# Five edits to a two-layer hybrid trunk: a later pump for the S5 sums, another PSUM pool, splits on another engine, compressed scores from split keys

## The chip, the core and the metric

The kernel runs on one core of one Trainium2 chip. Its engines have names in what follows: PE (TensorE, the matmuls; PEld is its weight load), DVE (VectorE), ACT (ScalarE), POOL (GpSimd) and SP (SyncE, which issues the DMAs). SBUF is the memory on the chip that the engines read and write, and PSUM, with eight banks, is where matmuls put their sums. The metric is the device time of one execution in microseconds (us).

## What is computed

Two layers of a decoder trunk, with a width of 1024 and 256 tokens. In each layer one input projection of the normed input feeds four token mixers; each mixer's output is gated, projected to 1024 and summed with the others:

```python
for l in range(DEPTH):
    h = rms_norm(x, norm_g[l])
    proj = h @ w_in[l]
    (nsa_q, nsa_kv, nsa_gate, nsa_z, sc_bcx, sc_z, sb_qkv, sb_z,
     s5_u, s5_z, merge) = jnp.split(proj, split_at, axis=-1)
    outs = (nsa_mixer(...) * jax.nn.silu(nsa_z), short_conv_mixer(...) * jax.nn.silu(sc_z),
            stick_breaking_mixer(sb_qkv) * jax.nn.silu(sb_z), s5_mixer(...) * jax.nn.silu(s5_z))
    gates = jax.nn.sigmoid(merge).reshape(b, s, N_MIXERS, D_MODEL)
    mixed = gates[:, :, 0] * (outs[0] @ w_branch[l, 0])
    for m in range(1, N_MIXERS):
        mixed = mixed + gates[:, :, m] * (outs[m] @ w_branch[l, m])
    x = x + mixed @ w_out[l]
```

Two of the mixers matter here. `nsa_mixer` is sparse attention; its compressed branch scores the queries against a few keys, each made of 32 tokens. `s5_mixer` is a complex linear recurrence over the 256 tokens, followed by a product with `c_re` and `c_im` that sums over the states. Weights and activations are float32.

## The kernel before

**Weights.** All projection weights come in 156 slots of 128x1024 (78 in each layer), in the order of use. SP issues one DMA for a slot (`raw`, three buffers). The slot is then split for products with more than one pass: `hi` is a cast to the format fp32r (L148, on ACT, for slots 17 and 87 on DVE), `lo` is `raw` minus `hi` (L150). The engine of L150 is DVE, save for the slots in the tuple `lo_pool`, where it is POOL. `hi` and `lo` have five buffers each. A product then has three passes: hi with hi, hi with lo, lo with hi, for the activations (`hh`, `hl`) as for the weights. `proj_n` (L488) and `proj_t` (L498) do so for 24 matmuls of 128x256 in each output bank or half bank.

**Stages of a layer.** First the slots of the queries and keys (`q`, `ksw`), the values `vsw`, the compressed keys `kvc`, the stick-breaking inputs (`sbq`, `sbk`, `sbv`), the S5 input `s5u` and the convolution's inputs; then merge gates (`mg`, four slots for each of eight blocks), SiLU gates (`z`) and the branch products (`br`, L943, one slot for each block) mixed as a list `TAIL` says, and at last the output product `wo`. A merge gate's tanh is L928 on ACT, and the gated branch products are the DVE operation `mt`, L946. POOL adds them up (L286).

**Order.** The mixers are Python generators. After each unit of projection the main program calls `pump()`, and every generator that isn't waiting is run on to its next `yield`; `yield n` sits out `n` pumps. So the code's order is that of the pumps. A scheduler with a model of the times then orders the instructions of PE, DVE and ACT, within what buffers and data allow. POOL and SP keep the order of the code.

**S5.** `s5` works on eight blocks of 128 states in a layer, two pairs with four blocks; a block is called a state below. For each state PE computes an input `bu`; DVE multiplies it with tables into `s5a` and `s5b` (L858, L859), POOL adds and subtracts halves (L286, L289), DVE scans along the tokens (L865, two scans), multiplies with the tables again into `cy` (L868, L871), POOL again subtracts and adds (L289, L286). After the four states of a pair comes a wait of two pumps and the sum over states, eight matmuls `s5acc` (L883). After the second pair come the weights of the last product (`gw`, a DMA, a cast and a subtraction on POOL) and the product `glu`. Names have the layer and the state at their end: `cy03` is state 3 of layer 0.

**PSUM pools.** `pj` has four banks, for projections; `wk` two, for mixers; `ac` two, for sums that live long (`s5acc` is one). Every projection of `n_part`, `ksw` too, takes a bank of `pj`.

**Compressed scores.** `nsa_compress` transposes the normed block-diagonal keys and copies them from PSUM as `bdkT`, in F32. `nsa_cmp` multiplies `hi` and `lo` of the queries with it: two matmuls for each of two token tiles and two head groups, eight in a layer, in F32 (L666).

## Time and profile before

| | before |
|---|---|
| three runs | 566.71, 568.88, 569.79 us (median 568.88) |
| the profiled execution | 566.94 us |
| its span, first to last instruction | 565.2 us |
| mean granted clock of PE, share of full speed | 0.987 |
| busy us: PE, DVE, ACT, POOL | 546.1, 440.1, 264.0, 275.3 |
| weight splits `lo` on DVE | 152, 209.1 us |
| weight splits `lo` on POOL | 4, 10.3 us |

All terms are worked out from the profiled execution, and 1.7 us of its time lie outside the span. The views that the prediction uses are: the busy shares of the engines (Rows 1), the list of PE's waits (Rows 2), which says who released PE after each wait, timelines of an engine over a few microseconds, and the busy time and granted clock of a stretch. In a timeline a row may stand for several like instructions ("x4"); the first number is the start of the first, the second the time from there to the end of the last. Matmuls overlap: a duration of 0.28 us is not what a matmul costs, that is the distance to the next start.

### The profile page before, as it was taken

Reading aid. Unit: us, or ns where it says so; the run is one execution under the profiler, and the core shown is the slowest. Engines: PE = TensorE matmul, PEld = TensorE weight load, DVE = VectorE, ACT = ScalarE, POOL = GpSimd, SP = SyncE. Lnnn points to the kernel's source line nnn. Section 1 sums busy time; section 2 is a strip of 40 time slices with the busy share of each in tenths; the row PEclk is TensorE's granted clock in tenths of the full one; section 3 lists DMA queues with packets and bytes.
Section 4 is the critical chain, followed back from the end, with each engine's and each line's share of the span. In section 5 each row is a group of like instructions: output and inputs, shape, how many; then the busy total and the mean of one; then the engine's idle time right before and its main releaser. Section 6 shows DMA issues by size and latency. Waiting matters only on the chain.

```text
span 565.2 us, 11178 instructions
## 1 busy us (share of the span) xinstructions
PE 546.1 (97%) x4417; PEld 510.1 (90%) x4417; DVE 440.1 (78%) x654; ACT 264.0 (47%) x436; POOL 275.3 (49%) x309
## 2 busy tenths in 40 slices
PE   6999999999899899799999999999999999999997
PEld 3898988889799799799998998889889999999997
DVE  3999776888989764888769985968898777687772
ACT  4656353654334444654454555454434345444440
POOL 7949536634665529597033776713335620243200
PEclk7899999999899999999999999999999999999999
DMA  7584154544444636465556725364344635555541
GB/s 257 194 279 157 42 201 119 199 153 146 150 126 137 223 134 206 149 199 180 190 171 213 220 72 164 112 222 135 112 154 147 202 139 180 187 188 186 188 135 53
DMA packets 28853, 93.54 MB, mean 166 GB/s; under 512 B 3968, under 2 KB 5248, under 8 KB 28800
## 3 DMA queue, kind: packets, MB, share of 16 engines
q1 hardware_dynamic: 28800, 92.82, 50.5%
q8 instruction: 35, 0.57, 0.4%
q14 instruction: 18, 0.15, 0.1%
HBM read 88.61 MB, written 1.05 MB: 159 GB/s over the span
## 4 chain that ended last, share of the span: by engine, by line
PE 71%; DVE 11%; POOL 9%; issue 4%; DMA 2%; ACT 2%; SPq 1%; DVEq 0%; POOLq 0%; ACTq 0%
PE mg L498 24%; PE wo L488 7%; PE br L943 7%; PE z L498 4%; DVE lo L150 2%; PE s5u L498 2%; PE sbv L488 2%; PE bg L498 2%; PE sc L709 2%; PE xin L498 2%; PE sbk L498 2%; PE nsacc L746 2%; DVE s5b L865 1%; POOL cy L286 1%; PE cg L498 1%
## 5 line engine op out<-in xcount | busy, mean ns | idle before, releaser
L150 DVE TENSOR_TENSOR lo<-raw,hi 128x1024 fp32r<-128x1024 f32 (+1 forms) x152 | 209.1, 1379 | 43.8 <-ACT hi L148 43.4
L148 ACT CAST hi<-raw 128x1024 fp32r<-128x1024 f32 (+1 forms) x154 | 161.2, 1050 | 173.8 <-PE mg L498 52.8
L498 PE MATMUL mg<-hh,hi 128*128 128x256 f32 x512 | 145.1, 283 | 0.4 <-DVE mt L946 0.4
L498 PE MATMUL mg<-hh,lo 128*128 128x256 f32 x512 | 144.6, 283 | 0.0
L498 PE MATMUL mg<-hl,hi 128*128 128x256 f32 x512 | 144.5, 282 | 0.0
L498 PEld LDWEIGHTS mg<-hh,hi 128*128 128x128 f32 x512 | 97.0, 190 | 3.0 <-issue 2.4
L498 PEld LDWEIGHTS mg<-hl,hi 128*128 128x128 f32 x512 | 97.4, 190 | 1.2 <-issue 1.2
L498 PEld LDWEIGHTS mg<-hh,lo 128*128 128x128 f32 x512 | 97.0, 189 | 1.2 <-issue 1.2
L286 POOL TENSOR_TENSOR mt<-mt,mt 128x512 f32<-128x512 f32 x12 | 19.0, 1585 | 70.6 <-DVE mt L946 70.6
L289 POOL TENSOR_TENSOR cy<-cy 128x256 f32<-128x256 f32 x16 | 18.2, 1138 | 57.9 <-DVE cy L871 54.2
L488 PE MATMUL wo<-hi,mx 128*128 128x256 f32 x256 | 45.6, 281 | 0.0
L488 PEld LDWEIGHTS wo<-hi,mx 128*128 128x128 f32 x256 | 39.2, 188 | 0.0
L943 PE MATMUL br<-oh,hi 128*128 128x256 f32 x128 | 36.0, 282 | 2.4 <-ACT g L928 2.4
L498 PE MATMUL z<-hh,hi 128*128 128x256 f32 x128 | 36.1, 282 | 0.0
L498 PE MATMUL z<-hl,hi 128*128 128x256 f32 x128 | 36.1, 282 | 0.0
L498 PE MATMUL z<-hh,lo 128*128 128x256 f32 x128 | 36.0, 281 | 0.0
L943 PE MATMUL br<-ol,hi 128*128 128x256 f32 x128 | 36.0, 281 | 0.0
L943 PE MATMUL br<-oh,lo 128*128 128x256 f32 x128 | 36.0, 281 | 0.0
L488 PE MATMUL wo<-lo,mx 128*128 128x256 f32 x128 | 35.3, 282 | 0.0
L865 DVE TENSOR_TENSOR_SCAN s5b<-r,s5a 128x256 f32<-128x256 f32 x32 | 20.3, 677 | 11.8 <-POOL s5a L289 11.8
L286 POOL TENSOR_TENSOR s5a<-s5a,s5b 128x256 f32<-128x256 f32 x16 | 20.2, 1262 | 17.1 <-DVE s5b L859 17.1
L943 PEld LDWEIGHTS br<-oh,hi 128*128 128x128 f32 x128 | 24.1, 189 | 2.6 <-ACT g L928 2.6
(333 smaller groups left out, 1417.4 us busy)
## 6 DMA issues: line engine op xcount, KB each, us to landing
raw<-in_ws_dram SPq DMA_DIRECT2D x152, 512.0 KB, 3.7
raw<-in_wq_dram SPq DMA_DIRECT2D x4, 536.0 KB, 5.0
w<-in_w_dram SPq DMA_DIRECT2D x4, 512.0 KB, 5.7
b<-bh SPq DMA_DIRECT2D x16, 64.0 KB, 2.0
u<-uh SPq DMA_DIRECT2D x16, 64.0 KB, 2.0
gw<-in_gw_dram SPq DMA_DIRECT2D x2, 512.0 KB, 5.4
out_dram<-xs SPq DMA_DIRECT2D x8, 128.0 KB, 1.7
xs<-in_x_dram SPq DMA_DIRECT2D x2, 256.0 KB, 3.2
```

Of the source, the lines that this page charges most:

```text
L148: self.nc.scalar.copy(hi[:, :w], t[:, :w])
L150: sub.tensor_sub(lo[:, :w], t[:, :w], hi[:, :w].bitcast(F32))
L286: G.tensor_add(o, a, b)
L289: G.tensor_sub(o, a, b)
L488: T.matmul(ps[:, :width], lhsT=act(4 * h + kk)[ia][:, tt], rhs=w[iw][:, kk, :], start=n == 0, stop=n == last)
L498: T.matmul(ps, lhsT=w[:, k, :], rhs=a[:, k, :], start=n == 0, stop=n == last)
L709: T.matmul(sc[kh].rearrange("p (b g k) -> p b g k", b=nb, g=2)[:, :, g, :], lhsT=qT[iq][rows[kh], g, t * P:(t + 1) * P], rhs=kT[ik][rows[k ...
L746: T.matmul(acc[rows[kh], :, t * P:(t + 1) * P], lhsT=v[:, c, b * P + 64 * kh:b * P + 64 * kh + 64], rhs=ps4[kh][:, c, 2 * i:2 * i + 2, :], ...
L865: V.tensor_tensor_scan(y[:, ri, :], L["r"][:, pr:pr + 1].to_broadcast([P, S]), a[:, ri, :], 0.0, op0=ALU.mult, op1=ALU.add)
L943: T.matmul(ps[:, j, :], lhsT=w[:, 2 * m + k, :], rhs=a[:, k, :], start=n == 0, stop=n == 5)
```

## The change

Five places of the code are changed.

1. `lo_pool` is empty: the splits of slots 4, 79, 81 and 95 are made by DVE.
2. `n_part` takes the bank of `ksw` from `ac`, of the others from `pj` as before.
3. `bdkT` becomes a pair of fp32r tiles, a rounded copy (ACT) and what the rounding leaves (one new subtraction of 128x64 on DVE).
4. The compressed scores are twelve fp32r matmuls in a layer, three passes, where eight F32 matmuls were.
5. In layer 0 the wait ahead of each pair's state sums is three pumps where two were; in layer 1 it stays at two (`3 - l`).

```diff
-    W = Weights(nc, tc, raw, hip, lop, wq, ws, 3, 5, (4, 79, 81, 95), (17, 87))
+    W = Weights(nc, tc, raw, hip, lop, wq, ws, 3, 5, (), (17, 87))
...
     def n_part(l, key, slots, act, t, done, width=256, by_pass=False):
-        ps = pj.tile([P, 512], F32, tag="pj", name=f"{key}{l}{t}")
+        pool, tag = (ac, "ac") if key == "ksw" else (pj, "pj")
+        ps = pool.tile([P, 512], F32, tag=tag, name=f"{key}{l}{t}")
...
-        bdkT = lp.tile([P, 64], F32, name=f"bdkT{l}", tag="bdkT")
-        A.copy(bdkT, pt[:, :64])
+        bdkT = tuple(lp.tile([P, 64], F32R, name=f"bdkT{i}{l}", tag=f"bdkT{i}") for i in range(2))
+        A.copy(bdkT[0], pt[:, :64])
+        V.tensor_sub(bdkT[1], pt[:, :64], bdkT[0].bitcast(F32))
...
-                for i in range(2):
-                    T.matmul(sc[:, t, g, :], lhsT=qT[i][:, g, t * P:(t + 1) * P].bitcast(F32), rhs=L["bdkT"], start=False,
-                             stop=t == g == i == 1)
+                for i, (iq, ik) in enumerate(PASSES):
+                    T.matmul(sc[:, t, g, :], lhsT=qT[iq][:, g, t * P:(t + 1) * P], rhs=L["bdkT"][ik], start=False,
+                             stop=t == g == 1 and i == 2)
...
-            yield 2
+            yield 3 - l
```

The scheduler answers with another order on PE, DVE and ACT. Three places of it carry the prediction. Lines of the code after stand one or two further down than before.

On PE, the last of the second pair's state sums in layer 0. `z30` is half of SiLU gate 3, which stands ahead of merge gate block 4 (`mg040`). Before:

```order
L498 MATMUL z30_2427<-hh0_154,hi45_2345 128x256
L498 MATMUL z30_2427<-hl0_155,hi45_2345 128x256
L883 MATMUL s5acc0_1977<-cy07_2268,CM_105 32x256
L883 MATMUL s5acc0_1977<-cy06_2183,CM_105 32x256
L498 MATMUL z30_2427<-hh0_154,lo45_2346 128x256
L498 MATMUL z30_2427<-hh0_154,hi45_2345 128x256
L498 MATMUL z30_2427<-hl0_155,hi45_2345 128x256
L498 MATMUL z30_2427<-hh0_154,lo45_2346 128x256
L883 MATMUL s5acc0_1977<-cy07_2268,CM_105 32x256
L498 MATMUL z30_2427<-hh0_154,hi45_2345 128x256
```

And after:

```order
L498 MATMUL z30_2412<-hh0_154,hi45_2351 128x256
L498 MATMUL z30_2412<-hl0_155,hi45_2351 128x256
L885 MATMUL s5acc0_2014<-cy07_2314,CM_105 32x256
L885 MATMUL s5acc0_2014<-cy06_2228,CM_105 32x256
L498 MATMUL z30_2412<-hh0_154,lo45_2352 128x256
L498 MATMUL z30_2412<-hh0_154,hi45_2351 128x256
L498 MATMUL z30_2412<-hl0_155,hi45_2351 128x256
L498 MATMUL z30_2412<-hh0_154,lo45_2352 128x256
L885 MATMUL s5acc0_2014<-cy07_2314,CM_105 32x256
L498 MATMUL mg040_2498<-hh0_154,hi46_2381 128x256
```

The grouping of the sums is as before, but the six `z30` products that stood behind the last sum now stand ahead of these three.

On ACT, the last tanh of merge gate 5 (`g05`, from the banks `mg050` and `mg051`) and the cosine and sine of layer 1's S5 tables (`cos1`, `sin1`). Before:

```order
L928 ACTIVATE g05_2716<-mg050_2717 128x512
L402 ACTIVATE cos1_2709<-sin1_2708 128x256
L403 ACT_TABLE_LOAD
L403 ACTIVATE sin1_2708<-sin1_2708 128x256
L404 ACTIVATE cos1_2709<-cos1_2709,halfpi_101 128x256
L148 CAST hi58_2859<-raw58_2760 128x1024
L148 CAST hi59_2897<-raw59_2795 128x1024
L928 ACT_TABLE_LOAD
L928 ACTIVATE g05_2716<-mg051_2790 128x512
L148 CAST hi60_2939<-raw60_2827 128x1024
```

And after:

```order
L930 ACTIVATE g05_2705<-mg050_2706 128x512
L148 CAST hi58_2860<-raw58_2755 128x1024
L148 CAST hi59_2900<-raw59_2793 128x1024
L930 ACTIVATE g05_2705<-mg051_2788 128x512
L402 ACTIVATE cos1_2783<-sin1_2782 128x256
L403 ACT_TABLE_LOAD
L403 ACTIVATE sin1_2782<-sin1_2782 128x256
L404 ACTIVATE cos1_2783<-cos1_2783,halfpi_101 128x256
L148 CAST hi60_2945<-raw60_2828 128x1024
```

The second tanh of `g05` now stands ahead of the tables' functions instead of behind them and behind a table load of its own.

On DVE, the end of state 3's chain in layer 0: `s5b03` is scanned, `cy03` is what POOL waits for, and `s5a06` and `s5b06` belong to the state that comes next. Before:

```order
L150 TENSOR_TENSOR lo40_2152<-raw40_2035,hi40_2151 128x1024
L858 TENSOR_TENSOR s5a06_2145<-bu06_2142,Ct0_600 128x512
L859 TENSOR_TENSOR s5b06_2146<-bu06_2142,St0_601 128x512
L150 TENSOR_TENSOR lo41_2195<-raw41_2077,hi41_2194 128x1024
L865 SCALAR_TENSOR_TENSOR s5b03_2068<-r0_157,s5a03_2067 128x256 x2
L868 TENSOR_TENSOR cy03_2106<-s5b03_2068,Ct0_600 128x512
L871 TENSOR_TENSOR cy03_2106<-s5b03_2068,St0_601 128x512
L150 TENSOR_TENSOR lo42_2237<-raw42_2113,hi42_2236 128x1024
```

And after:

```order
L150 TENSOR_TENSOR lo40_2146<-raw40_2037,hi40_2145 128x1024
L150 TENSOR_TENSOR lo41_2197<-raw41_2071,hi41_2196 128x1024
L867 SCALAR_TENSOR_TENSOR s5b03_2105<-r0_157,s5a03_2104 128x256 x2
L860 TENSOR_TENSOR s5a06_2181<-bu06_2178,Ct0_600 128x512
L861 TENSOR_TENSOR s5b06_2182<-bu06_2178,St0_601 128x512
L870 TENSOR_TENSOR cy03_2143<-s5b03_2105,Ct0_600 128x512
L873 TENSOR_TENSOR cy03_2143<-s5b03_2105,St0_601 128x512
L150 TENSOR_TENSOR lo42_2231<-raw42_2115,hi42_2230 128x1024
```

The two products of state 6 stand between the scan of state 3 and its products `cy03`; before they stood ahead of the scan, with a weight split between them and it. The same holds for state 7 and `cy06` further on.

## Rows read from the trace of the kernel before

**Rows 1.** Part 1 of the page: busy us, share of the span, instructions.
```profile
PE 546.1 (97%) x4417; PEld 510.1 (90%) x4417; DVE 440.1 (78%) x654; ACT 264.0 (47%) x436; POOL 275.3 (49%) x309
```

**Rows 2.** Waits of PE: in total, times, longest, in us.
```profile
PE ksw L488 <- DVE lo L150: 1.2, 1, 1.2
...
PE sc L709 <- ACT pTs L740: 0.8, 1, 0.8
...
PE sc L709 <- DVE qTl L601: 0.4, 1, 0.4
```

**Rows 3.** Timeline of PE, first state sum: start, us, work [idle <-releaser].
```profile
147.81 0.28 PE L498 MATMUL mg<-hl,hi 128*128 128x256 f32 x1
150.02 0.62 PE L883 MATMUL s5acc<-cy,CM 128*32 128x256 f32 x2 [1.93 <-POOL cy L289]
```

**Rows 4.** Windows: stretch, PE, PEld, DVE, ACT, POOL busy, granted clock, DMA.
```profile
151.00:154.40 3.40, 3.40 (x18) 3.40 (x17) 3.40 (x5) 1.55 (x3) 2.02 (x2) 0.51 0.58 186
```

**Rows 5.** Timeline of POOL, end of layer 0's last state.
```profile
192.25 1.71 POOL L286 TENSOR_TENSOR cy<-cy 128x256 f32<-128x256 f32 x1
```

**Rows 6.** Timeline of PE, the second half's state sums.
```profile
190.21 0.28 PE L498 MATMUL z<-hl,hi 128*128 128x256 f32 x1
192.33 0.63 PE L883 MATMUL s5acc<-cy,CM 128*32 128x256 f32 x4 [1.84 <-POOL cy L289]
...
194.00 0.62 PE L883 MATMUL s5acc<-cy,CM 128*32 128x256 f32 x2 [0.37 <-POOL cy L286]
...
195.36 0.28 PE L498 MATMUL mg<-hh,hi 128*128 128x256 f32 x1
...
195.95 0.28 PE L498 MATMUL mg<-hh,lo 128*128 128x256 f32 x1
```

**Rows 7.** Groups of DVE: count, busy us, mean ns, idle before them.
```profile
L150 DVE TENSOR_TENSOR lo<-raw,hi 128x1024 fp32r<-128x1024 f32 (+1 forms) x152 | 209.1, 1379 | 43.8 <-ACT hi L148 43.4
...
L859 DVE TENSOR_TENSOR s5b<-bu,St 128x512 f32<-128x512 f32 x16 | 10.9, 682 | 0.0
```

**Rows 8.** Timeline of ACT around the sine table of layer 1.
```profile
224.12 0.42 ACT L402 ACTIVATE cos<-sin 128x256 f32<-128x256 f32 x1 [2.36 <-POOL sin L289]
...
228.57 1.28 ACT L928 ACT_TABLE_LOAD   x1
229.86 0.60 ACT L928 ACTIVATE g<-mg 128x512 f32<-128x512 f32 x1
```

**Rows 9.** Timeline of PE, the same time.
```profile
227.84 0.28 PE L943 MATMUL br<-oh,lo 128*128 128x256 f32 x1
230.51 0.38 PE L943 MATMUL br<-oh,hi 128*128 128x256 f32 x1 [2.40 <-ACT g L928]
...
232.63 0.38 PE L498 MATMUL mg<-hh,hi 128*128 128x256 f32 x1 [0.43 <-DVE mt L946]
```

**Rows 10.** Timeline of DVE, beside two splits on POOL.
```profile
23.83 2.40 DVE L574 TENSOR_SCALAR ssq<-ssq 128x4 f32<-128x4 f32 x1
...
295.86 3.54 DVE L553 SCALAR_TENSOR_TENSOR h<-xs,ss,ng 128x512 f32<-128x512 f32 x2 [0.67 <-POOL ss L545]
```

**Rows 11.** Timeline of POOL, two of its four splits.
```profile
23.79 2.42 POOL L150 TENSOR_TENSOR lo<-raw,hi 128x1024 fp32r<-128x1024 f32 x1
...
295.80 2.39 POOL L150 TENSOR_TENSOR lo<-raw,hi 128x1024 fp32r<-128x1024 f32 x1
```

**Rows 12.** Timeline of PE, start of layer 1.
```profile
298.88 0.63 PE L561 MATMUL hT<-cs,h 128*128 128x128 f32 x4 [1.12 <-DVE h L553]
```

**Rows 13.** Timeline of PE, compressed scores of layer 1.
```profile
386.78 0.33 PE L666 MATMUL csc<-bdkT,qT 128*128 128x64 f32 x2
...
388.52 0.39 PE L830 MATMUL sbp<-cs,sbt 128*128 128x128 f32 x2
```

**Rows 14.** Timeline of PE, F32 products with 35 columns.
```profile
58.19 2.21 PE L614 MATMUL cy<-kc,w 128*64 128x35 f32 x62
```

**Rows 15.** Windows, DVE alone: stretch, DVE busy, granted clock, DMA.
```profile
22.00:48.00 26.00, 25.74 (x65) 1.00 0.71 238
```

## Prediction

> **What bounds the kernel now.** I read the shares of busy time first: TensorE (PE) works 546.1 us of a span of 565.2, that is 97% [rows 1]. Matmuls of 128x256 follow each other every 0.118 us (195.36 to 195.95 is five of them) [rows 6]. A change can therefore gain only in two ways: fewer or cheaper matmuls, or fewer pauses of PE. So I went on to the list of PE's waits and to the timeline around each. The time that a pause costs is the distance of the two starts less 0.118. The pauses that matter here are:
>
> - State sums of layer 0, which wait for the S5 chain on POOL: 147.81 to 150.02 costs 2.1 [rows 3], 190.21 to 192.33 costs 2.0, and up to 194.00 another 0.5 [rows 6]. After the first of them the granted clock is 0.51, the lower of its two levels, for 3.4 us: 18 matmuls [rows 4], which at 0.118 would take 2.1, so 1.3 are lost.
> - A branch product (`br`) that waits for ACT: 227.84 to 230.51 costs 2.55. ACT was busy with the sine of layer 1, and the tanh on which the PSUM bank hangs then needs its own table load of 1.28 [rows 8, 9]. The next gate product at 232.63 waits another 0.43 for DVE, about 0.6 with the longer first start [rows 9].
> - Starts of the layers: 1.2 for a weight split and 0.4 for `qTl` in layer 0, 0.8 for `pTs` in layer 1 [rows 2], and 1.12 for the last transposes of layer 1's input [rows 12].
>
> **The change part by part.**
>
> *State sums.* The edit is one number (one pump of delay less or more), but the order shows the last sums of layer 0 only six gate products later, 6 x 0.118 = 0.7 us. That cannot hide pauses of 2.0 and 0.5 whose cause is the chain itself: POOL's last addition for state 7 ends at 192.25 + 1.71 = 193.96 [rows 5], and the last sums start at 194.00 [rows 6]. So I ask what the change does to the chain. Its DVE order now has the two products of the next state (`s5a06`, `s5b06`, then 07) between the scan of a state and its two closing products. Each product takes 0.68 [rows 7], so each closing pair is 2 x 0.68 = 1.4 later; it is nearly full for state 3, about 1.0 for state 6 (a row of other work moved the other way), and at state 5 about 0.4 is won because `s5a02`, `s5b02` moved out of its way. Sum: the chain ends 1.3 + 1.0 - 0.4, about 2.0 later, near 196.0. The first gate product of block 4 stood at 195.36; of the 1.36 behind 194.00 the six products, 0.7, now come ahead of the sums, so it starts at 196.0 + 0.65 = 196.6: **+1.3**. Ahead of it PE has one short pause of 0.9, one near 156 of about 2.5 and one near 190 of about 4.3: the waits are moved and pooled, not removed. A pause of 2.1 was followed by the lower clock once [rows 4] and the one of 2.0 was not; for one of 4.3 I count it, at the same 1.3: **+1.3**. The half-speed stretch after the pause near 156 costs nothing, since PE then waits less for the chain. What is emitted with the sums moves as well: on SP the load of the last product's weights (`gw`) now stands behind two more slots, and layer 1's parameters behind the slot that they held up before; their readers, `glu`, stand 34 gate products (4.0 us) behind the sums, and I count nothing. Bounds: -5.9 (all of 2.1 + 2.0 + 0.5 + 1.3 gone) to +6 (twice my delay of the chain and the lower clock after both long pauses).
>
> *ACT at the end of layer 0.* By the order both tanh of gate 5 now run ahead of the sine of layer 1, so the bank is free as soon as its gate products are done. The 2.55 and the 0.6 go [rows 9]: **-3.1**. What is late next is the sine's own reader: it comes some 5 us later, and on DVE its first reader (`abi`, L442) now has `mt` of block 1 queued behind it, for which PE waits in turn; by my walk through the two orders `mt` has about 2.5 us left. Bounds: -3.1 to 0.
>
> *Weight splits to DVE.* Four splits leave POOL. One costs DVE 1.38 on average [rows 7]; on POOL it took 2.4 [rows 11]. So DVE takes on 4 x 1.4 = 5.5. Against that, DVE instructions stood still beside the POOL splits: a scaling of 128x4 took 2.40 and ended with the split beside it [rows 10, 11], where I take 0.2 from the size; the pair `h` took 3.54 beside the split at 295.80 [rows 10, 11]. At these two places what goes about makes up for what comes, in DVE time. For the PE it is better: the wait of layer 1's transposes shrinks from 1.12 [rows 12] by the shorter `h` and since twice as many `ksw` products now stand ahead of them (11 x 0.118 = 1.3 more cover), less the part of `h` that its new place behind two splits costs: **-0.6** (-1.1 to +0.7). In layer 1 the chain of the stick-breaking mixer is free of the POOL split of slot 95, and its transposed block stands behind 24 more products, so the 0.8 for `pTs` goes [rows 2]: **-0.8** (-0.9 to 0).
>
> The Trainium skill ("SBUF — State Buffer", section "Who interferes with whom") says that a DVE instruction with two SBUF inputs and a GpSimd (POOL) instruction that reads SBUF take one shared port pair in turns, the second waiting for the whole of the first. That speaks against this part too: a split on DVE then stops POOL for its length. The trace agrees that the second waits: 2.40 beside 2.42 [rows 10, 11]. By that rule the two placements are a gain, as I count them (-0.6, -0.8); by durations alone, 5.5 more on DVE, they would be the third rival below. By the rule the four splits would also cost POOL up to 4 x 1.4 = 5.5 and give DVE back up to 9.6, an estimate, and POOL's additions for the scores and norms near these places are the ones to watch.
>
> *Keys in the `ac` pool.* In layer 0 the `ksw` banks no longer block the `pj` pool, so value products start earlier and fill part of the 1.2 at the first split; and `qTl`'s wait goes [rows 2]. Of 1.6 I take a third: **-0.5** (-1.2 to +0.5, since DVE has no idle time there, 25.74 of 26.00 [rows 15]).
>
> *Compressed scores.* Before, 8 F32 products appear as 16 records, from 386.78 to 388.52, 0.109 each [rows 13]. After, 12 F32R products with the same 128-column weights. At 0.109 each they take 1.31 instead of 1.74: -0.43 a layer, **-0.85** in both. Bounds: if each still took two passes, 24 x 0.109 = 2.6, +0.9 a layer; if the cost went with columns, as the F32 products with 35 columns at 2.21 / 62 = 0.036 [rows 14], 12 x 0.036 = 0.4, -1.3 a layer. I take the middle since the weight load, not the columns, is like that of rows 13. The new subtraction on DVE of 128x64 is small and lies far ahead of its reader: nothing.
>
> **Sum.** +1.3 + 1.3 - 3.1 - 0.6 - 0.8 - 0.5 - 0.85 = -3.25. The profiled run took 566.94 us, so 563.7; the median of the runs shown lies 1.94 above the profiled one, so **565.6**.
>
> **The rivals.**
>
> *The state sums no longer wait.* If the new order of DVE ends the chain earlier than I walked, the pauses vanish: their term becomes -5.9 instead of +2.6, and the time is 563.7 - 8.5 = 555.2, with 1.94 about 557. For it: POOL idles between the states, DVE is not full. Against it: two products now stand in front of each closing pair. It decides at whether the last addition on POOL ends before PE is through with the products ahead of the sums. Chance 0.16.
>
> *The gain at ACT is given back.* If the merge products wait for the later S5 tables as long as the branch product did, the 3.1 goes and the time is 563.7 + 3.1 + 1.94 = 568.7: no change. Against it: those products have 2.5 us to spare. Chance 0.17.
>
> *DVE becomes the bound (slower).* At the start of layer 0 DVE is busy 25.74 of 26.00 us [rows 15]. If the instructions beside the POOL splits keep their length (because something else held them), the four splits add 5.5 to DVE and PE waits for it at each of the four places; the gains there, 0.6 + 0.8 + 0.5, go as well: 563.7 + 5.5 + 1.9 + 1.94 = 573.0, +0.7%. It decides at whether the 128x4 scaling falls from 2.40 to a few tenths. Against it: its end and that of the split beside it agree within 0.03. Chance 0.12.
>
> *The edit of the state sums does nothing.* If the sums hardly move and the chain too (+0), the time is 563.7 - 2.6 + 1.94 = 563.0, inside my range. Chance 0.12; the forecast itself keeps 0.43.
>
> **How the numbers follow.** Forecast 565.6. The lower end takes in the first rival, 557; the upper end lies at 571, between the forecast's own bad bound (the state sums at +6 instead of +2.6: 569.0) and the third rival, of which a part falls outside. About 0.5% (2.8 us: 566.0 to 571.7 is "the same") is what a measurement can tell from no change. Faster: 0.16 + 0.12 + half of 0.43, about 0.52. Slower: 0.12 + a little, 0.13. Same: 0.35.
>
> **What the profile after would show.** Right: no wait of `br` for ACT in the list; a pause of 2 to 3 us near 156 and one near 190 before sums, with the granted clock low after the latter; the 128x4 scaling at some 0.2; compressed scores with 12 records per layer at 0.11. Wrong: no state sum in the list of waits (first rival), a wait for `mt` or of `mg` for DVE near 230 (second), waits for `lo` at either start (third), or 24 records of the scores.

## The result and the profile after

The changed kernel takes **572.30 us** (median of 20 executions, 568.95 to 577.47). The kernel before, on the same chip, takes 568.92 (20 executions, 566.35 to 571.22). The ratio is **1.007, with a 95% interval of 1.0049 to 1.0091: slower by 0.7%**. I had forecast 565.6 and a range that ended at 571: wrong in sign and outside the range. (Here and below the ratio is not the quotient of the two medians; in the runs below the two differ by up to 0.18%.)

| | before | after |
|---|---|---|
| median, us | 568.92 | 572.30 |
| the profiled execution, us | 566.94 | 569.01 |
| its span, us | 565.2 | 567.2 |
| mean granted clock | 0.987 | 0.988 |

A caution for all that follows: the profiled execution of after is the second shortest of its twenty. The two traces differ by 2.1 us, the medians by 3.4. The traces can explain the first number only.

The page of after gives these busy shares, which answer to [rows 1]:

```profile
PE 545.3 (96%) x4409; PEld 507.9 (90%) x4409; DVE 443.2 (78%) x660; ACT 264.0 (47%) x436; POOL 267.0 (47%) x305
```

DVE has 3.1 us more and POOL 8.3 less. PE has the same work less eight records of the scores, in a longer span: it pauses more. The list of PE's waits in after (total, times, longest, in us) says where, beside [rows 2]:

```profile
PE s5acc L885 <- POOL cy L289: 8.1, 5, 2.8
...
PE sbp L832 <- DVE ce L677: 1.6, 1, 1.6
...
PE sc L711 <- ACT pTs L742: 1.1, 1, 1.1
...
PE pt L740 <- DVE ce L677: 0.5, 1, 0.5
...
PE br L945 <- ACT g L930: 0.2, 1, 0.2
```

The state sums (`s5acc`) wait five times where they waited twice; `sbp` and `pt` wait for the softmax of the compressed scores (`ce`), which nothing did before; `sc` waits longer for `pTs`; and the wait of `br` for ACT has gone from 2.4 to 0.2.

To see what each stage is worth I laid the same matmul of both traces side by side. The table gives the start of the first product into some banks and how much later it comes after; the last column says what lies between a mark and the one above it. (Where small products have changed sides of such a mark, the figure can be off by some tenths.)

| first product of | before, us | after comes later by | what lies between |
|---|---|---|---|
| `bg0` | 95.16 | -0.33 | start of layer 0 |
| `mg001` | 114.02 | -1.00 | compressed scores of layer 0 |
| `mg010` | 123.47 | +1.03 | softmax wait |
| `mg041` | 203.85 | +4.35 | state sums of layer 0 |
| `mg060` | 232.63 | +1.22 | the two tanh of gate 5 |
| `mg070` | 249.70 | +1.67 | |
| `ksw11` | 301.55 | +0.91 | start of layer 1 |
| `mg140` | 471.45 | +2.07 | all mixers of layer 1 |
| `wo131` | 559.13 | +2.09 | |

**The state sums of layer 0.** PE's timeline of after at the three places (start, us, work [idle <- releaser]), beside [rows 3, 6]:

```profile
151.04 0.62 PE L885 MATMUL s5acc<-cy,CM 128*32 128x256 f32 x2 [0.82 <-POOL cy L289]
...
156.18 0.28 PE L498 MATMUL mg<-hh,hi 128*128 128x256 f32 x1
158.93 0.96 PE L885 MATMUL s5acc<-cy,CM 128*32 128x256 f32 x4 [2.47 <-POOL cy L289]
...
193.25 0.28 PE L498 MATMUL z<-hl,hi 128*128 128x256 f32 x1
196.36 0.85 PE L885 MATMUL s5acc<-cy,CM 128*32 128x256 f32 x4 [2.83 <-POOL cy L289]
```

These are the places that I had named (0.9, about 2.5 near 156, about 4.3 near 190). The second cost 2.63, as told; the third, near 193, cost 2.99 and not 4.3. Two stretches at the lower clock follow, one after each; I had expected both and priced the second alone. The windows give the length, then PE, PEld, DVE, ACT and POOL, then the granted clock:

```profile
159.00:162.00 3.00, 3.00 (x11) 1.22 (x11) 1.70 (x3) 0.00 (x0) 2.84 (x3) 0.51 0.66 194
196.60:199.80 3.20, 3.20 (x12) 1.63 (x9) 0.41 (x2) 2.09 (x2) 2.44 (x2) 0.51 0.78 262
```

Why the chain was late is seen on DVE and POOL. The last state of layer 0 in after, first DVE, then POOL:

```profile
189.26 1.27 DVE L867 TENSOR_TENSOR_SCAN s5b<-r,s5a 128x256 f32<-128x256 f32 x2 [0.63 <-POOL s5a L289]
190.46 1.20 DVE L150 TENSOR_TENSOR lo<-raw,hi 128x1024 fp32r<-128x1024 f32 x1
191.57 0.68 DVE L780 TENSOR_TENSOR ol<-zt,oh 128x512 fp32r<-128x512 f32 x1
192.17 0.68 DVE L870 TENSOR_TENSOR cy<-s5b,Ct 128x512 f32<-128x512 f32 x1
192.78 0.68 DVE L873 TENSOR_TENSOR cy<-s5b,St 128x512 f32<-128x512 f32 x1
193.38 2.35 DVE L150 TENSOR_TENSOR lo<-raw,hi 128x1024 fp32r<-128x1024 f32 x2
```
```profile
193.60 2.71 POOL L289 TENSOR_TENSOR cy<-cy 128x256 f32<-128x256 f32 x1 [4.37 <-PE z L498]
196.28 0.72 POOL L286 TENSOR_TENSOR cy<-cy 128x256 f32<-128x256 f32 x1
```

A weight split and a product of other work stand between the scan and the closing products (190.46 to 192.17, 1.7 us), and then the first POOL operation takes 2.71, while the next one of the same size, with no split beside it, takes 0.72. It ends 0.6 after the second of the two splits, so it seems to have stood still for both. The chain ends at 196.28 + 0.72 = 197.0, which is 3.0 later than in [rows 5]; 1.0 of it was there at `mg010` already.

**The softmax wait.** PE and DVE of after around 113 us:

```profile
113.49 0.28 PE L498 MATMUL mg<-hl,hi 128*128 128x256 f32 x1
115.36 0.52 PE L832 MATMUL sbp<-cs,sbt 128*128 128x128 f32 x3 [1.59 <-DVE ce L677]
```
```profile
112.50 0.41 DVE L672 TENSOR_REDUCE cmx<-csc 128x8 f32<-128x256 f32 x1
112.83 1.42 DVE L150 TENSOR_TENSOR lo<-raw,hi 128x1024 fp32r<-128x1024 f32 x1
114.17 0.58 DVE L673 TENSOR_SCALAR cmx<-cmx 128x8 f32<-128x8 f32 x1
114.79 0.42 DVE L677 TENSOR_TENSOR ce<-csc,cmx 128x256 f32<-128x256 f32 x1
```

The split of slot 26 now stands between the maximum of the scores and its scaling, and PE waits 1.87 - 0.12 = 1.75 for the subtraction behind it. (Whether that split is the cause is tested below; it is not the whole of it.)

**Layer 1.** Here the wait for `pTs`, which I had counted as gone, is 1.14 instead of 0.75 [rows 2], and the last state sums wait three times:

```profile
367.24 0.38 PE L711 MATMUL sc<-kT,qT 64*128 64x256 f32 x1 [1.14 <-ACT pTs L742]
...
449.30 0.40 PE L885 MATMUL s5acc<-cy,CM 128*32 128x256 f32 x1 [1.05 <-POOL cy L289]
...
457.63 0.63 PE L885 MATMUL s5acc<-cy,CM 128*32 128x256 f32 x4 [0.91 <-POOL cy L289]
...
459.30 0.62 PE L885 MATMUL s5acc<-cy,CM 128*32 128x256 f32 x2 [0.26 <-POOL cy L286]
```

The three cost 1.21 + 1.07 + 0.42 = 2.7; before, the one pause in this stretch cost 0.2. On ACT of after the engine sits waiting for `sbt` (5.30) and then has the cast `uh` in front of the copy, which costs the copy 366.60 - 366.11 = 0.49. In the trace of before the copy came first, but it too was released by `sbt`, after 5.46:

```profile
366.11 0.59 ACT L1076 CAST uh<-s5u 128x512 fp32r<-128x512 f32 x1 [5.30 <-DVE sbt L826]
366.60 0.59 ACT L742 COPY pTs<-pt 128x512 f32<-128x512 f32 x1
```

### The profile page after: what moved, and what is told of

Read it like the earlier page. It is cut to its first block, busy times and chain, and to the rows that moved or that the text cites. A ratio compares the mean times of both kernels' runs of the same rounds, so it can differ in the third digit from the quotient of the medians.

```text
span 567.2 us, 11171 instructions
## 1 busy us (share of the span) xinstructions
PE 545.3 (96%) x4409; PEld 507.9 (90%) x4409; DVE 443.2 (78%) x660; ACT 264.0 (47%) x436; POOL 267.0 (47%) x305
## 4 chain that ended last, share of the span: by engine, by line
PE 62%; DVE 10%; POOL 8%; DMA 6%; issue 6%; SPq 4%; ACT 3%; DVEq 0%; POOLq 0%; ACTq 0%
PE mg L498 23%; PE wo L488 8%; PE br L945 6%; PE z L498 6%; DMA raw<-in_ws_dram 5%; SPq L212 3%; DVE lo L150 2%; PE kvc L498 2%; PE sbq L498 2%; PE vsw L488 2%; ACT hi L148 2%; PE ksw L488 2%; PE q L488 2%; POOL cy L289 2%; PE s5acc L885 1%
## 5 line engine op out<-in xcount | busy, mean ns | idle before, releaser
L150 DVE TENSOR_TENSOR lo<-raw,hi 128x1024 fp32r<-128x1024 f32 (+1 forms) x156 | 212.7, 1368 | 47.2 <-ACT hi L148 46.7
L498 PEld LDWEIGHTS z<-hl,hi 128*128 128x128 f32 x128 | 24.3, 190 | 0.8 <-issue 0.8
```

Of the source, the lines that this page charges most:

```text
L150: sub.tensor_sub(lo[:, :w], t[:, :w], hi[:, :w].bitcast(F32))
L498: T.matmul(ps, lhsT=w[:, k, :], rhs=a[:, k, :], start=n == 0, stop=n == last)
```

## The experiments

All ratios are to the kernel before, measured on the same chip in the same stretch (its medians were 568.29 to 568.34), with 95% intervals. "Order edge" means that one instruction is told to stand behind another on the same engine; it adds no semaphore and no work, but the scheduler may move other instructions in answer.

Each run left one trace as well. This table lays some of them on the marks of the table above; each figure is how much longer a stretch took than in the rows' execution, in us. The first line is the kernel before itself in a second execution, so a difference of its size need not come from an edit.

| run | up to `mg010` | `mg010` to `mg060` | `mg060` to `ksw11` | `ksw11` to `mg140` | in all, at `wo131` |
|---|---|---|---|---|---|
| `r_before` | -0.40 | +2.93 | -0.05 | -0.82 | +1.67 |
| after | +1.03 | +0.19 | -0.31 | +1.17 | +2.09 |
| `e1_only_y` | -0.95 | +0.75 | +0.25 | +5.14 | +5.19 |
| `j3_y_chain` | +0.11 | -0.84 | +0.02 | +5.08 | +4.37 |
| `e2_late2` | -0.43 | -1.08 | +0.54 | +3.13 | +2.16 |
| `g3_late_chain` | -0.67 | +0.21 | +0.53 | +2.73 | +2.79 |
| `e3_undo_y` | +2.81 | +3.07 | -0.70 | +0.77 | +5.97 |
| `f3_chain` | +0.68 | -2.15 | -0.57 | +2.80 | +0.78 |
| `f2_tanh_first` | +0.18 | -0.64 | +0.06 | -0.71 | -1.12 |

From `mg010` to `mg060` lie the state sums of layer 0 and the wait of `br` for ACT, from `ksw11` to `mg140` the mixers of layer 1.

### The parts apart

*The later pump alone.*

```diff
-            yield 2
+            yield 3 - l
```

> Only the later pump of the state sums in layer 0, all else as before. Theory A (what the changed kernel's trace suggests): the edit does two things that nearly cancel, a longer S5 chain in layer 0 (+3.3 us, pauses ahead of the sums near 157 and 195 with low clock after them) and the tanh of gate 5 ahead of the sine (-3.1), so the profiled run is within 1 us of the kernel before up to 250 us, and what comes on top is in layer 1, at the S5 sums near 450. Theory B (the loss belongs to the four splits on DVE): this kernel, which keeps them on POOL, is faster than before by 1 us or more.

Measured: 572.26 us, **1.0062** [1.0042, 1.0082]. So this one number alone loses nearly as much as all five edits, and it also carries the gain at ACT: the list of waits no longer has `br`. Theory A was right about the place: up to `mg070` the trace is level with the rows (+0.06), and the loss comes in layer 1. In the trace the last sums of layer 0 wait 3.06, which the gain at ACT nearly makes up for (+3.59 up to `mg041`, -2.84 from there to `mg060`), and a new wait of 2.78 stands in layer 1, where the edit leaves the number at two:

```profile
458.30 0.62 PE L883 MATMUL s5acc<-cy,CM 128*32 128x256 f32 x4 [2.78 <-POOL cy L289]
```
```profile
454.94 3.31 POOL L289 TENSOR_TENSOR cy<-cy 128x256 f32<-128x256 f32 x1 [4.37 <-DVE cy L871]
```

The granted clock falls behind this wait (0.64 from 458 to 461). From the first product of `mg130` to that of `mg131`, the same 54 products of PE take 11.49 where they took 7.29: 4.2 of the 5.1 us of layer 1 lie here.

*The other edits without the pump.* Edits 1 to 4, `yield 2` kept.

> The changed kernel with the pump of the state sums put back. Theory A: the S5 pauses of layer 0 are those of before (2.1, 2.0, 0.5), the branch product waits 2.55 again, and the wait of the scores' softmax near 113 (1.75) stays, since the four splits on DVE cause it; sum against before about -1.0 + 1.75 - 0.8 = 0, within 1.5 us. Theory C (the later pump is the loss): 3 us faster than the changed kernel.

Measured: 572.86 us, **1.0081** [1.0053, 1.011]. The two halves don't add up: each alone is as slow as both together. Theory A named the pauses rightly, but its sum fails, since the time isn't near that of before; theory C fails too, since it isn't below that of after. The trace of this run shows a wait of `sbp` for the softmax of 2.11 near 117 and one for `pTs` of 1.44 near 371; both are in after as well. Against `r_before`, the other execution that has long sums in layer 0, it is longer by 1.40 up to `bg0`, by 2.51 at the softmax wait and by 1.59 in the mixers of layer 1, and shorter by 0.7 at the scores and 0.7 at the start of layer 1.

*The four splits alone.*

```diff
-    W = Weights(nc, tc, raw, hip, lop, wq, ws, 3, 5, (4, 79, 81, 95), (17, 87))
+    W = Weights(nc, tc, raw, hip, lop, wq, ws, 3, 5, (), (17, 87))
```

> The kernel before with the four splits of slots 4, 79, 81, 95 on DVE and nothing else. Theory A: one split (slot 26) moves between the maximum and the subtraction of the compressed softmax and PE waits for it near 113, +1.75; the starts of the layers gain some 1 us as in the changed kernel; within 1.5 us of before. Theory B (DVE becomes the bound): 3 us or more slower, with waits of PE for splits at both layer starts.

Measured: 568.85 us, **1.0003** [0.9979, 1.0027]. DVE takes on the splits without a loss or a gain that can be measured. The split of slot 26 stands between the maximum and its scaling here too, and yet `sbp` doesn't wait: DVE ran 1.3 us earlier there (the subtraction starts at 113.53, in after at 114.79), and PE reached `mg001` some 3 us later. So this place has little slack, and it takes a late DVE as well as the split to show.

*The splits with one of the other two edits.* `j1_lo_ksw` is edits 1 and 2, `j2_lo_csc` is edits 1, 3 and 4.

> The kernel before with the four splits on DVE and ksw in the ac pool; scores and pump as before. Theory (the pool carries the loss: other banks at the start of both layers change the order of all that follows): about 1.007, with the softmax wait of about 2 us near 114 and a wait of sc for pTs near 370 of over 1 us. Rival (the scores carry it, since they change when the softmax can start): 1.000, and neither wait is over 1 us.

> The kernel before with the four splits on DVE and the twelve products of split keys; ksw and pump as before. Theory (the pool carries the loss): 0.999, by the 0.8 us that the scores save, and no wait over 1 us of sbp for ce. Rival (the scores carry it): about 1.007, with the wait of about 2 us near 114.

Measured: with the pool 567.11 us, **0.9982** [0.9966, 0.9997]; with the scores 570.85 us, **1.0029** [1.0007, 1.005]. The theory that the pool carries the loss has fallen, although the trace of `j1_lo_ksw` has the softmax wait (1.18 at 115.39): that wait alone doesn't make this kernel slower. With the scores the kernel is 0.3% slower than before, but against the splits alone (1.0003) the difference is inside the errors. The trace shows a longer wait for `pTs`, with the cast `uh` long done (it started at 360.00):

```profile
366.94 0.38 PE L710 MATMUL sc<-kT,qT 64*128 64x256 f32 x1 [1.56 <-ACT pTs L741]
```

Whatever is taken for the parts, they don't reach the 0.8% of `e3_undo_y`: the rest comes only when all are in.

### The gain at ACT by itself

The kernel before, with one order edge on ACT: the first function of layer 1's tables (the absolute value of the cosine's argument, L402) behind the second tanh of gate 5.

```diff
+    edges = [("abs1", "g051")]
...
+                tc.add_manual_dep(marks[later], marks[earlier].name,
+                                  mybir.DependencyInfo(mybir.DependencyClass.NoSync, mybir.DependencyReason.DATA),
+                                  reason="issue order")
```

> The kernel before with one edge in ACT's order: the sine of layer 1 stands behind the second tanh of gate 5. PE's and POOL's order are those of before, word for word; DVE moves ten small operations. My theory: the wait of the branch product for ACT (2.55) and the 0.6 behind it go and come back nowhere, -3.1 us. Rival: the S5 tables of layer 1 come later and PE waits for them, so the gain is given back in the same stretch, 0.

Measured: 565.82 us, **0.9943** [0.9918, 0.9967]: -3.2 us by the ratio (-1.9 to -4.7 by its interval, -2.5 by the medians), where the sum had -3.1. The timeline of ACT, against [rows 8]: the tanh at 226.20 has no table load ahead of it, and the tables' functions follow it.

```profile
226.20 0.59 ACT L939 ACTIVATE g<-mg 128x512 f32<-128x512 f32 x1
226.80 0.42 ACT L413 ACTIVATE cos<-sin 128x256 f32<-128x256 f32 x1
227.23 1.28 ACT L414 ACT_TABLE_LOAD   x1
```

Of the second rival (the gain is given back at `mt`) there is a trace: PE waits 1.16 for `mt` at 232.17, where it was 0.43 [rows 9]. That is 0.7 more, against the 2.55 that went, and from `mg041` to `mg060` the trace is 1.92 shorter, not 3.1: a part of the gain is given back, and that the ratio meets the sum so closely is partly luck. If the later pump gains as much at this place, it loses about 0.62 + 0.57 = 1.2%, some 6.8 us, elsewhere; that is an estimate from two ratios.

### The chain of states in layer 0

The changed kernel, with six order edges on DVE: the products of states 6 and 7 and the splits of slots 44 and 47 behind the closing products of the states whose chains they delay.

```diff
+    edges = [("a06", "cy03"), ("b06", "cy03"), ("a07", "cy06"), ("b07", "cy06"), ("lo44", "cy06"), ("lo47", "cy07")]
```

> The changed kernel with six edges on DVE in layer 0: the products of the next state (06 and 07) and two weight splits stand behind the closing products of the state ahead (03, 06, 07). My theory: the chain ends about 2 us earlier, the pause near 193 shrinks from 3.0 to about 1 and the low clock behind it goes, 2 to 3.5 us faster than the changed kernel. Rival: the chain is set by POOL's operations beside splits on DVE, and the order of DVE's products matters little, less than 1 us.

Measured: 568.20 us, **1.000** [0.9972, 1.0028], against 1.007. The pause near 193 is down from 2.99 to 1.27 (with a second of 0.42 behind it), and the clock behind it stays high (window with length, PE, PEld, DVE, ACT, POOL, clock):

```profile
191.47 0.28 PE L509 MATMUL z<-hl,hi 128*128 128x256 f32 x1
192.85 0.63 PE L896 MATMUL s5acc<-cy,CM 128*32 128x256 f32 x4 [1.10 <-POOL cy L300]
```
```profile
193.00:196.00 3.00, 2.73 (x19) 1.71 (x15) 1.70 (x3) 0.00 (x0) 1.47 (x1) 1.00 0.97 381
```

By the table the stretch from `mg010` to `mg060` is 2.3 shorter than in after, and the mixers of layer 1 are 1.6 longer.

The same six edges on the later pump alone:

> The kernel before with the later pump alone, and the six order edges of f3_chain in layer 0. Theory (the later pump loses some 4 us in layer 0's chain of states): 1.0062 - 0.007 = 0.999, with the pause near 193 at 1 to 1.5 us in place of 3.3 and no low clock behind it. Rival (its loss lies in layer 1, at the pause of 2.94 near 455): 1.005 or more, with that pause still there.

Measured: 569.38 us, **1.0024** [1.0000, 1.0047], against 1.0062: 2.2 us of the loss go by the ratios, whose intervals just overlap, and PE's wait near 193 falls from 3.06 to 1.36. The wait in layer 1 stays at 2.76 (457.48), and the low clock behind it too. Both theories hold in part. In the traces the order of layer 0's chain brings 1.6 back (+0.75 to -0.84), and layer 1 keeps its 5.1: the larger part of what the pump loses lies there, 4.2 of it at the last state sums.

Two chain edges on the kernel before, with the edge on ACT:

```diff
+    edges = [("abs1", "g051"), ("lo44", "cy06"), ("lo47", "cy07")]
```

> The kernel before with three edges: the sine of layer 1 behind the second tanh of gate 5 (0.57% faster alone), and in layer 0 the splits of slots 44 and 47 behind the closing products of states 06 and 07. My theory: the chain is what the pause near 190 waits for, so it shrinks from 2 to 3 us to about 1, and the time falls by another 1 to 2 us, some 0.8 to 0.9% faster than before in all. Rival: the splits go elsewhere into the chain's way, or POOL's operations run beside them instead, and the time is that of the first edge alone.

Measured: 565.55 us, **0.995** [0.9924, 0.9976], the same as the ACT edge alone. With the order of before, these two edges bring nothing that can be measured.

### How much one order of instructions varies

The kernel before once more, one execution:

> The kernel before once more, for a second trace. If the pauses ahead of the state sums of layer 0 (2.1, 2.0, 0.5) repeat within 0.3 us, the differences of the pauses between two traces can be read as effects of the edits. If they move by 1 us or more with the same order of instructions, only those beyond that can.

Measured: 568.6 us, span 566.8, 1.6 more than the execution of the rows. Nothing in the order is different, yet the last sums wait 2.98 instead of 1.84 [rows 6], and the clock falls behind them, which it did not in the execution that I had worked from:

```profile
193.03 0.63 PE L883 MATMUL s5acc<-cy,CM 128*32 128x256 f32 x4 [2.98 <-POOL cy L289]
```
```profile
193.40:196.60 3.20, 3.20 (x16) 2.07 (x13) 0.87 (x2) 0.00 (x0) 2.58 (x2) 0.64 0.74 243
```

DVE and POOL of this run show why:

```profile
190.05 2.35 DVE L150 TENSOR_TENSOR lo<-raw,hi 128x1024 fp32r<-128x1024 f32 x2
```
```profile
190.27 2.71 POOL L289 TENSOR_TENSOR cy<-cy 128x256 f32<-128x256 f32 x1 [4.37 <-DVE cy L871]
```

And the same place in the execution of the rows:

```profile
190.48 2.88 DVE L150 TENSOR_TENSOR lo<-raw,hi 128x1024 fp32r<-128x1024 f32 x2
```
```profile
190.71 1.57 POOL L289 TENSOR_TENSOR cy<-cy 128x256 f32<-128x256 f32 x1 [4.38 <-DVE cy L871]
```

In the execution of the rows POOL got in between the two splits (it took 1.57, and the pair of splits 2.88); in this one it stood still for both (2.71, and the pair took 2.35). That is 1.1 us by who comes first, but the next POOL operation took 0.73 here where it took 1.71 [rows 5], so the chain ends at 193.67, no more than 0.1 later when both traces are counted from `mg010`. The stretch from `mg010` to `mg041` is 2.24 longer all the same. So nearly all of it is the low clock behind one pause of 3.1, where the execution of the rows had two, of 2.0 and 0.5, and kept its clock.

### The softmax wait

The changed kernel, with the split of slot 26 behind the subtraction:

```diff
+    edges = [("lo26", "ce0")]
```

> The changed kernel with one edge on DVE: the split of slot 26 stands behind the subtraction of the compressed softmax of layer 0, not between the maximum and it. My theory: the wait of the transposes for the softmax near 113 (1.75) goes, 1.0 to 1.8 us faster than the changed kernel. Rival: the softmax was late for other reasons (its maximum started late), and the wait falls by less than 0.5.

Measured: 569.95 us, **1.001** [0.9975, 1.0046]. The rival was right about the place: the wait is still 1.78.

```profile
115.70 0.52 PE L843 MATMUL sbp<-cs,sbt 128*128 128x128 f32 x3 [1.78 <-DVE ce L688]
```
```profile
112.85 1.64 DVE L150 TENSOR_TENSOR lo<-raw,hi 128x1024 fp32r<-128x1024 f32 x1
114.41 0.41 DVE L683 TENSOR_REDUCE cmx<-csc 128x8 f32<-128x256 f32 x1
...
115.13 0.42 DVE L688 TENSOR_TENSOR ce<-csc,cmx 128x256 f32<-128x256 f32 x1
```

Without the split in between, the maximum itself starts 1.9 later than in after, behind another split: DVE as a whole is late there. Yet the median is 2.35 us below that of after, and no pause that I could see accounts for it (its profiled execution, 570.92, is longer than after's). The edge also moved small products on PE: nine more stand between `bg0` and `mg001` than in after. So a change of 0.6% can come without a visible cause, which also limits what `f3_chain` proves: its pause went as told, but its trace is only 1.3 us shorter than that of after, where the medians differ by 4.1.

### Layer 1, and the time at which its tables are prepared

The one link from edit 5 to layer 1 that I found is that layer 1's tables are prepared when the last S5 sums of layer 0 are through, so a pump later. The kernel before with only this moved (two pumps later):

```diff
         L["y3"] = th
+        yield 2
         spawn(prepare(l + 1))
```

> The kernel before, with the tables of layer 1 (the sine) prepared two pumps later and nothing else: the S5 order of layer 0 stays as before, the tanh of gate 5 comes ahead of the sine. Theory A: the wait of the branch product (2.55) and the 0.6 behind it go, -3.1 up to 240 us, the pauses near 148 and 190 stay as before; layer 1's S5 sums near 450 may lose up to 2.5. Rival: the order of ACT was not the cause of that pause, which then stays, 0.

Measured: 570.49 us, **1.0024** [1.0000, 1.0049]. The wait of `br` for ACT is down to 0.3; if that is worth what it was alone (0.9943), the move loses some 0.8% elsewhere. The trace loses 3.13 in the mixers of layer 1, 2.7 of it from `mg130` to `mg131`, where it has a wait of 2.79, with the same signature on POOL and DVE as in `e1_only_y`:

```profile
453.40 3.31 POOL L289 TENSOR_TENSOR cy<-cy 128x256 f32<-128x256 f32 x1 [4.38 <-DVE cy L871]
```
```profile
453.18 0.69 DVE L778 TENSOR_TENSOR ol<-zt,oh 128x512 fp32r<-128x512 f32 x1
453.78 2.35 DVE L150 TENSOR_TENSOR lo<-raw,hi 128x1024 fp32r<-128x1024 f32 x2
```

POOL starts beside `ol`, and then both splits are ahead of it. The granted clock stays at 1.00 behind this wait (457 to 460), where it fell in `e1_only_y`. So a shift of layer 1's tables is enough to bring this wait; that it is the whole of what the pump does to layer 1 is not shown.

The same with two edges that keep the splits of slots 120 and 121 behind the closing products:

```diff
+    edges = [("lo120", "cy17"), ("lo121", "cy17")]
```

> The kernel with the tables of layer 1 prepared two pumps later, plus two edges on DVE in layer 1: the splits of slots 120 and 121 stand behind the closing products of state 17, the last of that layer. My theory: the pause of 2.8 us ahead of the last state sums of layer 1 near 455 came from a split between the two closing products and from POOL's operations beside two more; it shrinks to about 1, and the kernel is 1 to 2 us faster than the one without the edges (which was 0.24% slower than before). Rival: the later tables are late for the whole of layer 1 and the pause stays above 2.

Measured: 569.34 us, **1.001** [0.998, 1.004]. In the trace the pause shrinks from 2.96 to 0.93, a second of 0.53 and a wait of 0.26 for `s5y` come behind it; from `mg130` to `mg131` 1.6 us are won in the trace. In time it is 0.14%, inside the error: that the pause is worth its length is so not shown.

### The edits without the later pump and without the loss

The kernel before with the edge on ACT, `ksw` in `ac`, and the scores from split keys (edits 2, 3, 4):

> The kernel before with the edge on ACT (0.57% faster alone), the keys in the other PSUM pool and the compressed scores from split keys; the splits stay on POOL and the state sums at two pumps. It tells which of the three edits makes the changed kernel without the later pump slow (0.81% slower than before, though the four splits alone were 0.03%). If the pool of the keys or the scores do it, this kernel is at least 0.3% slower than the one with the edge alone; if it takes the splits on DVE together with them, it is as fast or 0.2% faster.

Measured: 565.77 us, **0.9941** [0.9915, 0.9967], which is the edge alone. Edits 2 to 4 cost nothing and bring nothing measurable when the splits stay on POOL.

The edge on ACT, the two chain edges and the split scores (edits 3 and 4):

> As the kernel with three edges, plus the compressed scores from split keys (edits 3 and 4 of the change), without its other edits. My theory: the twelve fp32r products save 0.4 us a layer, so 0.8 us (0.15%) faster than with the three edges alone. Rival: the new order that the scheduler makes around the scores costs as much or more, as in the changed kernel (a wait for the softmax near 113).

Measured: 564.51 us, **0.9939** [0.9914, 0.9963]. This has the lowest median of all, but it can't be told from `f2_tanh_first` and `h1_ksw_scores`: the one edge on ACT, which all three have, is enough to beat the kernel before by 0.6%.

## Why the prediction was wrong

**State sums of layer 0 (+2.6): right in mechanism, too small by 0.7, and on a lucky base.** The three pauses stand where the order said. Counted from `mg010`, the chain ends 2.0 later (197.0 - 194.0 less the 1.03 that had come before), as walked, and six products stand ahead of the last sums: +1.3, as priced. But the whole term is +3.3 in the traces (from +1.03 to +4.35 in the table), so 2.0 are left for the low clock behind the pause, priced at 1.3. And `r_before` shows that the order of before can have this low clock too (+2.24 in the same stretch), which the execution of the rows had missed: against `r_before` the term is +1.1. I set the sum against the rows' own 566.94, so the base fits; but a trace of one execution priced a term that varies by more than 2 us from one to the next.

**ACT (-3.1): right.** -3.13 in the traces, -2.84 in that of `e1_only_y`. Alone, in `f2_tanh_first`, it is -3.2 by the ratio but -1.92 in the trace, where 0.7 more of a wait for `mt` comes back.

**Compressed scores (-0.85): right in size, not seen in the time.** Of after, the last of twelve records per layer starts 1.22 behind the first: 1.22 / 11 = 0.11 each, as taken.

```profile
384.37 0.39 PE L668 MATMUL csc<-bdkT,qT 128*128 128x64 f32 x2
...
385.59 0.28 PE L668 MATMUL csc<-bdkT,qTl 128*128 128x64 f32 x1
```

By the distances of their starts, all records of `csc` in both layers take 2.85 where they took 3.70. But together with the splits the kernel was slower than before by 0.3% (`j2_lo_csc`), and with the splits on POOL the edit can't be told from none (`h1_ksw_scores`).

**Splits to DVE (-0.6 at the start of layer 1): right there.** -0.76 in the table, and the same within 0.02 in all six other traces that have this edit, at most 0.04 either way in those that don't; `h` there takes 1.41 where it took 3.54 [rows 10]. The 128x4 scaling, which took 2.40, takes 0.16:

```profile
L575 DVE TENSOR_SCALAR ssq<-ssq x1: 158/158/158, 27.0 to 27.0; 128x4 f32<-128x4 f32 x1
```

So the third rival, DVE as the bound at 573.0, came nearest in time and is wrong as a mechanism: over 22 to 48 us DVE is busy 24.25 of 26.00, less than before [rows 15], and the splits alone cost nothing (1.0003). The cost went in part to the other side: `r` (128x8) on POOL took 1.67 with no split beside it in before (at 26.16) and takes 2.64 with one beside its start. The Trainium skill ("SBUF — State Buffer", section "Who interferes with whom") states that a DVE instruction with two SBUF inputs contends with a GpSimd instruction that reads SBUF; the trace agrees, with 1.0 us more for `r`.

```profile
23.29 2.64 POOL L388 TENSOR_TENSOR r<-ebase,lrdt 128x8 f32<-128x8 f32 x1
```

**`pTs` (-0.8): a failed step.** I took the wait to go since POOL is free and more products stand ahead. But in both traces what releases the copy on ACT is `sbt` on DVE, and in the new order of ACT the cast `uh` stands in front of the copy as well (0.49); I hadn't read ACT there. The result is +0.4 instead of -0.8. That `uh` is not the whole of it shows in `j2_lo_csc`, where it is out of the way and the wait is 1.56. And `r_before` has no wait for `pTs` at all: the 0.8 that I counted on was itself not there in a second execution.

**`ksw` in `ac` (-0.5): not shown.** `bg0` starts 0.33 earlier, which looks about right. But in `r_before`, without this edit, it starts 0.40 earlier, and in `e1_only_y` 0.95. The wait for `qTl` is gone from the list, as told; `ksw` waits 1.7 for splits where it waited 1.2.

**What the sum left out: the failed step that decides the sign.** I priced the pauses that the trace of before shows, and the three places at which I had read the order. Three more places in the table lose what I counted at nothing: the softmax wait of layer 0 (+2.0 from `mg001` to `mg010`), 0.45 behind `mg060`, and layer 1's mixers. There the state sums pause for 2.5 more, `pt` for 0.7 and `sc` for 0.4 more; the scores give 0.4 back, and the net is +1.2, so 2.0 come back in small pieces. Of these I can place 0.6 (the twenty products `sbz`, grouped in another way, take 2.96 instead of 3.56, by the distances of their starts). With these the table adds up: -0.33 - 0.67 + 2.03 + 3.32 - 3.13 + 0.45 - 0.76 + 1.16 + 0.02 = +2.09. The forecast of -3.25 missed this by 5.3: 2.0, 0.45 and 2.4 (with `pTs` in it) lie at these three places, 0.7 at the state sums of layer 0.

A caution on such sums: the stages aren't independent. In `e4_only_lo` the stretch of the state sums is 3.28 longer than in the rows, and the wait of `br` for ACT behind it shrinks from 2.40 to 0.86; a pause ahead of a fixed wait is partly taken back by it. Where an edit removes that wait, as here, nothing takes it back at that place.

**What stays open.** Why edits 1 to 4 together cost 0.8%, when 1 costs 0.0, 1 and 2 -0.2, 1, 3 and 4 +0.3, and 2 to 4 nothing. The trace of `e3_undo_y` says where (start of layer 0, softmax wait, layer 1), not by what. Also open is why the last state sums of layer 1, which cost the later pump alone 4.2 us, pause for less in after, and how much of the last 1.3 us between the traces' difference and the medians' is more frequent standing still of POOL: the longer spread of after (8.5 us against 4.9) would go with it, but one trace of each can't show it.

## What to carry to other kernels

When a scheduler orders the instructions, an edit of one pump reorders the whole program: compare the old and the new order at every place where an engine is within a microsecond or two of the bound, not only at the waits that the trace shows. If an edit's gain is a side effect of its new order (here, the tanh ahead of the tables), ask for that order directly: one edge brought 0.6%, where the edit that had it as a by-product lost 0.6%. And take a second trace of the same kernel before pricing a pause, since what varies between the two is the least error of the sum: here it had a low clock more and the wait for `pTs` less.

## What the runs showed of the hardware

A POOL operation of 128x256 with two inputs took 0.72 to 0.74 alone, 1.57 to 1.73 where it started beside one weight split on DVE, 2.71 beside two in a row, 3.31 beside a product and two splits, and 3.84 beside three splits in a row (`j3_y_chain` at 189.90). I had expected one split's length at most. Which of the two engines goes first after the first split isn't fixed by the order of the instructions: the same kernel had 1.57 in one execution and 2.71 in another.

After pauses of about 2 us on PE the granted clock fell in some places and executions and not in others: 0.51 after 2.1 [rows 3, 4], full speed after 2.0 by the starts in [rows 6]. After 1.27 in `f3_chain` it stayed at 1.00. After the pauses of 2.6 and 3.0 in after it fell both times, and after the one of 3.1 in `r_before` too (0.64 over the stretch shown). Of two equal pauses at the same place in layer 1 (2.94 and 2.96, start to start less 0.118), it fell behind that of `e1_only_y` (0.64) and stayed at 1.00 behind that of `e2_late2`; the same 54 products around it took 11.49 and 10.01.
